# Local attention: the key and query norm roots are emitted one projection tile after their sums, the key root's broadcast another tile on

## The chip, the cores and the metric

The kernel runs on one core of a Trainium2 chip. The metric is device time in microseconds (us) from launch to end, lower is better. The inputs are float32; products run on TensorE in pieces (a rounded high part and the remainder), so each product of two matrices is three matmuls.

## What is computed

The reference is a two-layer encoder trunk over 16 meta tokens and 1024 tokens. The part that matters here is the local (windowed) attention of the first layer: 8 query heads in 2 key groups, each head of width 128, with an RMS norm of every query and key row before the attention.

```python
def swa_mixer(q_s, k_s, v_s, g_qn, g_kn, sink, cos, sin):
    ...
    q = apply_rope(rms_norm(q, g_qn), cos, sin)
    k = apply_rope(rms_norm(k, g_kn), cos, sin)
    q = q.reshape(B, SWA_KV_HEADS, SWA_REP, T, SWA_HEAD_DIM)
    o = banded_window_attention(q, k, v, sink, SWA_HEAD_DIM ** -0.5)
```

The kernel does not norm the rows before the rotation. It rotates the raw projections, sums their squares over the head's 128 features on TensorE, takes the root of the sums, and multiplies it in later: the key root as a full row over the rotated keys, the query root as a column that scales the scores.

## The kernel before

The residual stream lies transposed, features on the partitions and 1040 tokens along the free dimension. The stage of interest begins at line 524. A projection tile is `proj1(e)` (line 273): 128 output features, two halves of the weights, 36 matmuls a half, into three PSUM banks that have one buffer each in this stage. The next tile can start on a bank only when the tile before has been copied out of it. `tick()` is called inside `proj1`, behind the matmuls of the second half: it counts down the list `todo` and emits what `put_off(n, fn)` laid in it n ticks earlier. `flush()` (line 215) ticks until the list is empty.

`k_prep(g)` (line 546) projects the keys of a group: copy out of PSUM (L327, ScalarE), square (L552), scale by the norm weights on GpSimd (L553), `stat` (line 178, high and low part of the squares; its `later()` holds the sum on TensorE L197, the copies L198 and the store L199 to a row in DRAM), and `rope` (line 402: two loads of the swapped halves L405 and L406, then three full-width multiplies and adds L407 to L409). `q_prep(u)` (line 619) does the same for two heads, folds the squares of both (L439, L440, L641), and casts each rotated head to its high and low part (L633, L634).

The root of a key row is `row_rsqrt` (line 319): load the sums as 16 x 65 (L321), add the epsilon (L322), eleven small VectorE instructions of a Newton iteration (L136 to L141), store (L324). `fin2` (line 561) then loads the root broadcast to 128 partitions (`rkb`, L152) and multiplies the keys by it (L563); `put` makes the keys' high and low parts (L570 to L573). The root of a query pair is `fin` in `q_prep` (line 644): four small loads (L148, L297), L651, the same iteration on 128 x 17, and L653; the scores instruction (L694) reads the result.

Full-width rows in this stage come from one pool tag `T` with four buffers: the raw projections `kraw` and `qraw`, the swapped halves `sw`, the copied sums `sr`, the broadcast root `rkb`, and the gate rows `gt` and `gth`.

The order of emission is v, keys of group 0, query pair 0, gate tile 0, `flush()`, `put` of group 0; then 36 units of attention (four pairs of nine blocks) with the remaining projection tiles pulled in between them, 4.6 credit a unit against 5.3 a half tile (line 816: query pair 1, gate 1, query pair 2, keys of group 1, gate 2, query pair 3, gates 3 to 9). `flush()` and the `put` of group 1 stand ahead of unit 18.

The framework that builds the program chooses the order of each engine's queue at compile time. The emission order is the priority in that choice, no fixed order: the scales of the other attention (emitted behind gate tile 0) and the `put` of group 0 stand in the trace ahead of work that was emitted before them. A buffer of a tag is handed out in its own order.

Of the kernel before, what the change touches and what calls it, by code (L numbers as in the profile page):

```python
# [41 lines left out]
def trunk_kernel(ctx: ExitStack, tc: tile.TileContext, a: dict, out: bass.AP):  # L42
# [29 lines left out]
    def row(nm, tag, dt=F32, w=T):  # L72
        if tag == "X":
            return xapool.tile([P, T], dt, tag="X", name=nm)
        return sb["P"].tile([P, w], dt, tag=tag, name=nm, bufs=sb["cnt"][tag])
# [5 lines left out]
    def vcol(j):  # L81
        return vec[:, j:j + 1]
# [49 lines left out]
    def newton_rsqrt(v, shape, nm):  # L132
        y = small.tile(shape, F32, tag="nw_y" + nm, name="nw_y", bufs=1 if nm in ("72", "65", "9") else 2)
        t = small.tile(shape, F32, tag="nw_t" + nm, name="nw_t", bufs=1)
        yi = y.bitcast(I32)
        nc.vector.tensor_scalar(yi, v.bitcast(I32), 1, None, ALU.logical_shift_right)  # L136
        nc.vector.tensor_scalar(yi, yi, -1, 1597463007, ALU.mult, ALU.add)
        for _ in range(3):
            nc.vector.tensor_mul(t, y, y)
            nc.vector.scalar_tensor_tensor(t, t, -0.5, v, ALU.mult, ALU.mult)  # L140
            nc.vector.scalar_tensor_tensor(y, t, 1.5, y, ALU.add, ALU.mult)  # L141
        return y
# [4 lines left out]
    def tok_load(dst, r):  # L147
        nc.sync.dma_start(dst, r[NM:T].rearrange("(i p) -> p i", p=P))  # L148

    def bcast_row(r, nm, tag):  # L150
        t = row(nm, tag)
        nc.sync.dma_start(t, r.to_broadcast([P, T]))  # L152
        return t
# [24 lines left out]
    def stat(sq, s, m, dst, tag=None, rt="S"):  # L178

        hi = row("sqh", rt, F32R)  # L180
        lo = row("sql", rt, F32R)
        nc.gpsimd.tensor_scalar(hi, sq, 1.0, 1.0, ALU.mult, ALU.mult)
        nc.vector.tensor_sub(lo, sq, hi.bitcast(F32))

        def later():
            sr = row("sr", "T")
            if tag is None:
                ps = big("st")
                for j, x in enumerate((hi, lo)):
                    for c0, c1 in CH:  # L190
                        nc.tensor.matmul(ps[:m, OFF + c0:OFF + c1], s, x[:, c0:c1], start=j == 0, stop=j == 1)
                nc.scalar.copy(sr[:m], ps[:m, OFF:OFF + T])
            else:
                for c0, c1 in C3:
                    ps = bank("st", tag)
                    for j, x in enumerate((hi, lo)):
                        nc.tensor.matmul(ps[:m, :c1 - c0], s, x[:, c0:c1], start=j == 0, stop=j == 1)  # L197
                    nc.scalar.copy(sr[:m, c0:c1], ps[:m, :c1 - c0])  # L198
            nc.sync.dma_start(dst, sr[:m])  # L199

        return later
# [3 lines left out]
    def put_off(n, fn):  # L205
        todo.append([n, fn])
# [66 lines left out]
    def proj1(e):  # L273
        ps = parts("pj")
        for hf in range(2):
            wh, wl = split_w(a["w1"][e, hf], (4, P), "w1")
            mm3p(ps, [(wh[:, k], wl[:, k], xh[4 * hf + k], xl[4 * hf + k]) for k in range(4)], hf == 0, hf == 1)
            if hf == 1:
                tick()
            yield 5.3 if hf == 0 else ps  # L280
# [15 lines left out]
    def meta_col(dst, r):  # L296
        nc.sync.dma_start(dst, r[0:NM].unsqueeze(1))  # L297
# [21 lines left out]
    def row_rsqrt(src, n, dst):  # L319
        t16 = small.tile([16, 65], F32, tag="t16", name="t16", bufs=2)  # L320
        nc.sync.dma_start(t16, flat(src))  # L321
        nc.vector.scalar_tensor_tensor(t16, t16, 1.0 / n, e16, ALU.mult, ALU.add)  # L322
        y16 = newton_rsqrt(t16, [16, 65], "16")
        nc.sync.dma_start(flat(dst), y16)  # L324

    def take(ps, r, dve=False):
        evac(ps, lambda t, c: nc.vector.tensor_copy(r[:, c], t) if dve else nc.scalar.copy(r[:, c], t))  # L327
# [74 lines left out]
    def rope(raw, half, C, S, tag="T", eng=nc.vector):  # L402
        sw = row("sw", tag)
        for b in range(0, P, 2 * half):
            nc.sync.dma_start(sw[b:b + half], raw[b + half:b + 2 * half])  # L405
            nc.sync.dma_start(sw[b + half:b + 2 * half], raw[b:b + half])  # L406
        eng.tensor_mul(sw, sw, S)  # L407
        nc.vector.tensor_mul(raw, raw, C)
        nc.vector.tensor_add(raw, raw, sw)  # L409
# [27 lines left out]
    def fold(r, j, t0, t1):  # L437

        nc.scalar.activation(t0[64 * j:64 * j + 64], r[0:64], AF.Square)  # L439
        nc.scalar.activation(t1[64 * j:64 * j + 64], r[64:128], AF.Square)  # L440
# [97 lines left out]
    def steps(g, res):  # L538

        for v in g:  # L540
            if isinstance(v, float):
                yield v
            else:
                res.append(v)

    def k_prep(g):
        o = []
        yield from steps(proj1(6 + g), o)
        raw = row("kraw", "T")
        take(o[0], raw)  # L550
        sq = row("ksq", "S")
        nc.scalar.activation(sq, raw, AF.Square)  # L552
        nc.gpsimd.tensor_scalar(raw, raw, vcol(V_SK), 1.0, ALU.mult, ALU.mult)  # L553
        sk = stat(sq, one, 1, d_sk[g], "s")
        rope(raw, 64, sC, sS, eng=nc.gpsimd)

        def fin():
            sk()
            row_rsqrt(d_sk[g], 128, d_rks[g])

        def fin2():
            rkb = bcast_row(d_rks[g], "rkb", "T")
            nc.vector.tensor_mul(raw, raw, rkb)  # L563

        def put():
            kh = swa.tile([P, NB, 144], F32R, tag="kh", name="kh")
            kl = swa.tile([P, NB, 144], F32R, tag="kl", name="kl")
            real = raw[:, NM:T].rearrange("p (b c) -> p b c", b=NB)
            meta = raw[:, 0:NM].unsqueeze(1).to_broadcast([P, NB, NM])
            nc.scalar.copy(kh[:, :, NM:144], real)  # L570
            nc.scalar.copy(kh[:, :, 0:NM], meta)
            nc.vector.tensor_sub(kl[:, :, NM:144], real, kh[:, :, NM:144].bitcast(F32))
            nc.vector.tensor_sub(kl[:, :, 0:NM], meta, kh[:, :, 0:NM].bitcast(F32))  # L573
            KV[g, "k"] = (kh.rearrange("p b c -> p (b c)"), kl.rearrange("p b c -> p (b c)"))

        put_off(1, fin)
        put_off(2, fin2)
        KV[g, "put"] = put
        yield 5.3

# [38 lines left out]
    def q_prep(u):  # L619
        qs = []  # L620
        t0, t1 = row("qs0", "S"), row("qs1", "S")
        meta = swa.tile([P, 2, 32], F32R, tag="qm", name="qm", bufs=2)
        for r in range(2):
            o = []
            yield from steps(proj1(8 + 2 * u + r), o)
            raw = row("qraw", "T")
            take(o[0], raw)
            fold(raw, r, t0, t1)
            nc.gpsimd.tensor_scalar(raw, raw, vcol(V_SQ), 1.0, ALU.mult, ALU.mult)
            rope(raw, 64, sC, sS, eng=nc.gpsimd if u else nc.vector)  # L630
            h = row("sqh_", "q", F32R)
            lo = row("sql_", "q", F32R)
            nc.scalar.copy(h, raw)  # L633
            nc.vector.tensor_sub(lo, raw, h.bitcast(F32))  # L634
            nc.scalar.copy(meta[:, 0, NM * r:NM * r + NM], raw[:, 0:NM])
            nc.vector.tensor_sub(meta[:, 1, NM * r:NM * r + NM], raw[:, 0:NM],
                                 meta[:, 0, NM * r:NM * r + NM].bitcast(F32))
            qs.append((h, lo))
            if r == 0:
                yield 5.3  # L640
        nc.gpsimd.tensor_add(t0, t0, t1)  # L641
        sq2 = stat(t0, sel, 2, d_sq[u], "s")

        def fin():
            sq2()
            sc = small.tile([P, 17], F32, tag="ssc", name="ssc", bufs=2)
            nc.vector.memset(sc[:, 16:17], 1.0)
            for r in range(2):
                tok_load(sc[:, 8 * r:8 * r + 8], d_sq[u][r])
                meta_col(sc[NM * r:NM * r + NM, 16:17], d_sq[u][r])  # L650
            nc.vector.scalar_tensor_tensor(sc, sc, 1.0 / 128, evx_s, ALU.mult, ALU.add)  # L651
            y = newton_rsqrt(sc, [P, 17], "17")
            nc.vector.tensor_scalar(sc, y, 128.0 ** -0.5, None, ALU.mult)  # L653
            QQ[u] = (qs, meta, sc)

        put_off(1, fin)
        yield 5.3

    class Unit:
# [151 lines left out]
    for _ in chain(v_prep(), k_prep(0), q_prep(0), gate_tile(0)):  # L811
        pass
# [373 lines left out]
    class Lru:  # L1186
# [87 lines left out]
        def root(self):  # L1274
            tz = self.tz
            nc.scalar.activation(tz, tz, AF.Sqrt, scale=0.25)
# [358 lines left out]
```

## Time and profile before

| | us |
|---|---|
| median of three timed runs | 1867.83 (1867.34 to 1867.99) |
| the profiled execution's own time | 1866.78 |
| its span, first to last instruction | 1864.9 |
| TensorE busy in the span | 1803.3 (97%) |
| VectorE busy | 1229.8 (66%) |
| ScalarE busy | 877.3 (47%) |
| GpSimd busy | 802.1 (43%) |

A row of a timeline reads: start, duration, engine and line, operation, output and input names, shapes, and in brackets the idle time of that engine just before with what ended it. In a table by stretches each engine has its busy time and its instruction count, PEclk is the granted TensorE clock as a share of full speed. PEld is the weight load of TensorE, SPq the queue that issues DMAs.

### The profile page before, as it was taken

The page shows a single profiled execution, that of the slowest core. Times are in us where ns is not written, and L with a number is a line of the kernel's source. Part 1 is how long each engine was busy: PE and PEld are TensorE (multiplying, and loading weights), DVE is VectorE, ACT ScalarE, POOL GpSimd, SP SyncE. Part 2 cuts the span into 40 slices and gives each one's busy share as a digit, 9 for nine tenths or more (in the row PEclk, how much of TensorE's full clock was granted, in tenths as well). Part 3 has the DMA queues.
Part 4 walks back from the last instruction along what each step waited for, and adds up shares of the span by engine and source line. Part 5 has one row for each costly group of instructions (what it writes and reads, how often), then busy time and mean ns, then how long its engine had stood idle before and what let it go on. Part 6 is the DMA issues. An engine that isn't in the chain of part 4 may idle for free.

```text
span 1864.9 us, 28561 instructions
## 1 busy us (share of the span) xinstructions
PE 1803.3 (97%) x10822; PEld 1641.8 (88%) x10822; DVE 1229.8 (66%) x1956; ACT 877.3 (47%) x1490; POOL 802.1 (43%) x713
## 2 busy tenths in 40 slices
PE   8999989989999999999999999999999999999999
PEld 7997888889999999888888889998888889988887
DVE  8687357787764641678777774348988989989000
ACT  5455224445443210466667652127776676674000
POOL 5446365354322463357555433332433433326331
PEclk9999999999999999999999999999999999999999
DMA  5355532223222363323222103422222222136421
GB/s 181 81 191 185 164 92 69 62 60 103 61 84 93 137 184 115 117 69 93 70 75 75 41 24 117 145 70 60 76 80 74 95 72 77 60 131 254 143 77 41
DMA packets 109333, 186.47 MB, mean 100 GB/s; under 512 B 31951, under 2 KB 51535, under 8 KB 109198
## 3 DMA queue, kind: packets, MB, share of 16 engines
q1 hardware_dynamic: 109198, 184.67, 31.2%
q8 instruction: 85, 1.39, 0.3%
q14 instruction: 50, 0.41, 0.1%
HBM read 126.72 MB, written 49.92 MB: 95 GB/s over the span
## 4 chain that ended last, share of the span: by engine, by line
PE 69%; DVE 16%; ACT 7%; POOL 5%; issue 2%; DMA 1%; SPq 0%; DVEq 0%; POOLq 0%; ACTq 0%
PE pj L168 12%; PE oo L168 10%; PE pxop L168 6%; PE pg L1183 5%; PE px L935 5%; PE pu L1183 5%; PE av L1026 4%; PE tp L998 3%; PE op L168 3%; PE up L168 3%; PE pz L128 2%; PE vps L435 2%; PE py L935 2%; DVE oxl L769 1%; DVE oz L1287 1%
## 5 line engine op out<-in xcount | busy, mean ns | idle before, releaser
L116 POOL TENSOR_TENSOR wl<-wr,wh 128x512 fp32r<-128x512 f32 (+2 forms) x218 | 320.8, 1475 | 301.9 <-ACT wh L113 269.8
L115 POOL TENSOR_SCALAR wh<-wr 128x512 fp32r<-128x512 f32 (+2 forms) x157 | 121.6, 775 | 376.0 <-PE pj L168 124.4
L168 PE MATMUL pj<-xh,wl 128*128 128x346 f32 (+1 forms) x768 | 251.3, 328 | 14.3 <-DVE wl L116 7.8
L168 PE MATMUL pj<-xl,wh 128*128 128x346 f32 (+1 forms) x768 | 249.1, 324 | 0.9 <-DVE xl L269 0.8
L168 PE MATMUL pj<-xh,wh 128*128 128x346 f32 (+1 forms) x768 | 248.9, 324 | 0.0
L168 PEld LDWEIGHTS pj<-xh,wl 128*128 128x128 f32 x768 | 146.5, 191 | 16.1 <-ACT xh L268 7.7
L168 PEld LDWEIGHTS pj<-xl,wh 128*128 128x128 f32 x768 | 146.6, 191 | 2.0 <-DVE xl L269 1.9
L168 PEld LDWEIGHTS pj<-xh,wh 128*128 128x128 f32 x768 | 146.6, 191 | 0.1
L1183 PE MATMUL pu<-h1h,wl 128*128 128x346 f32 (+1 forms) x384 | 125.2, 326 | 6.3 <-DVE ou L1201 3.3
L1183 PE MATMUL pu<-h1l,wh 128*128 128x346 f32 (+1 forms) x384 | 123.5, 322 | 0.0
L1183 PE MATMUL pu<-h1h,wh 128*128 128x346 f32 (+1 forms) x384 | 123.4, 321 | 0.0
L1013 ACT CAST pth<-tp 128x512 fp32r<-128x512 f32 (+1 forms) x160 | 77.9, 507 | 66.2 <-PE tp L998 52.3
L1014 DVE TENSOR_TENSOR ptl<-tp,pth 128x512 fp32r<-128x512 f32 (+1 forms) x160 | 90.2, 585 | 19.9 <-ACT pth L1013 16.4
L1183 PE MATMUL pg<-h1h,wl 128*128 128x512 f32 x256 | 101.4, 396 | 0.0
L168 PE MATMUL oo<-oyh,wh 128*128 128x512 f32 x256 | 101.1, 395 | 0.0
L1183 PE MATMUL pg<-h1h,wh 128*128 128x512 f32 x256 | 101.1, 395 | 0.0
L1183 PE MATMUL pg<-h1l,wh 128*128 128x512 f32 x256 | 100.8, 394 | 0.0
L168 PE MATMUL oo<-oyh,wl 128*128 128x512 f32 x256 | 100.6, 393 | 0.0
L168 PE MATMUL oo<-oyl,wh 128*128 128x512 f32 x256 | 100.4, 392 | 0.0
L944 ACT ACTIVATE p<-py,mmx,msc 128x256 f32<-128x256 f32 (+1 forms) x72 | 40.8, 567 | 119.0 <-DVE mmx L942 102.3
L1351 DVE TENSOR_TENSOR hres<-oo,hres 128x512 f32<-128x512 f32 x16 | 10.6, 688 | 129.0 <-PE oo L168 129.0
L998 PE MATMUL tp<-ident,p 128*128 128x128 f32 (+1 forms) x576 | 90.5, 275 | 2.7 <-POOL p L955 1.9
(446 smaller groups left out, 5471.2 us busy)
## 6 DMA issues: line engine op xcount, KB each, us to landing
wr<-in_w SPq DMA_DIRECT2D x128, 256.0 KB
wr<-in_wo SPq DMA_DIRECT2D x64, 256.0 KB
s_g<-gth SPq DMA_DIRECT2D x10, 520.0 KB
xr<-in_x SPq DMA_DIRECT2D x8, 520.0 KB
s_qn<-qr SPq DMA_DIRECT2D x8, 520.0 KB
s_kn<-kr SPq DMA_DIRECT2D x8, 520.0 KB
sw<-qraw SPq DMA_DIRECT2D x16, 260.0 KB
yb<-s_yb SPq DMA_DIRECT2D x8, 520.0 KB
```

The source lines that it names most:

```text
L115: eng.tensor_scalar(hi[:, :n], raw[:, :n], 1.0, 1.0, ALU.mult, ALU.mult)
L116: eng.tensor_sub(lo[:, :n], raw[:, :n], hi[:, :n].bitcast(F32))
L128: nc.tensor.matmul(ps[:m, off + c0:off + c1], w, x[:, c0:c1], start=first and j == 0 and pi == 0, stop=last and j == nt - 1 and pi == 2)
L168: nc.tensor.matmul(t[:, :c1 - c0], w, x[:, c0:c1], start=first and j == 0 and pi == 0, stop=last and j == nt - 1 and pi == 2)
L435: nc.tensor.matmul(ps[:m, :n], s, w, start=j == 0 and pi == 0, stop=j == nt - 1 and pi == 2)
L935: nc.tensor.matmul(dst[:m, d0:d0 + a1 - a0], l[:, s], r[:, a0:a1], start=pi == 0, stop=pi == 4)
L944: nc.scalar.activation(p_[:m, b0:b1], ps, AF.Exp, bias=mx[:m, 2:3], scale=sc, accum_out=mx[:m, 3 + z:4 + z])
L998: nc.tensor.transpose(tp[:, o:o + m], p_[:m, NM + P * (kt + j):NM + P * (kt + j) + P], ident[:m, :m])
L1013: nc.scalar.copy(hi[:, :w], tp[:, :w])
L1014: nc.vector.tensor_sub(lo[:, :w], tp[:, :w], hi[:, :w].bitcast(F32))
L1026: nc.tensor.matmul(av[:, :n], l[:, vs], pts[kt][o][:, j * n:j * n + n], start=kt == 0 and j == 0 and pi == 0, stop=False)
L1183: nc.tensor.matmul(t[:, :c1 - c0], l, r[:, c0:c1], start=hf == 0 and k == 0 and pi == 0, stop=hf == 1 and k == 3 and pi == 2)
```

## The change

For the keys, `fin` (sums and root together, one tick later) is split: the sums stay one tick later, the root comes two ticks later, and the broadcast with its product moves from two ticks to three. For the queries, the sums stay one tick later and the loads, the root and its scaling move to two ticks. No instruction is added or removed.

```diff
-        def fin():
-            sk()
+        def root():
             row_rsqrt(d_sk[g], 128, d_rks[g])
...
-        put_off(1, fin)
-        put_off(2, fin2)
+        put_off(1, sk)
+        put_off(2, root)
+        put_off(3, fin2)
...
         def fin():
-            sq2()
             sc = small.tile([P, 17], F32, tag="ssc", name="ssc", bufs=2)
...
-        put_off(1, fin)
+        put_off(1, sq2)
+        put_off(2, fin)
         yield 5.3
```

## Rows read from the trace of the kernel before

**Rows 1.** Table by stretches of the stage and of what follows it: stretch, its length, busy time and instruction count of each engine, granted clock, DMA share, GB/s.
```profile
250.00:300.00 50.00, 42.70 (x257) 40.54 (x257) 32.67 (x67) 17.28 (x38) 24.04 (x20) 0.97 0.30 81
...
400.00:450.00 50.00, 46.17 (x314) 44.38 (x313) 40.50 (x108) 24.61 (x69) 19.23 (x24) 1.00 0.36 95
...
500.00:550.00 50.00, 49.70 (x340) 48.91 (x339) 31.54 (x89) 21.12 (x62) 15.16 (x23) 1.00 0.26 80
```

**Rows 2.** TensorE's timeline where query pair 0 is projected: the last matmul into the first PSUM bank of its second head, the last of that head, and the two tile starts behind it that waited.
```profile
255.56 0.32 PE L168 MATMUL pj<-xh,wh 128*128 128x348 f32 x1
...
259.38 0.32 PE L168 MATMUL pj<-xh,wh 128*128 128x346 f32 x1
264.03 0.43 PE L168 MATMUL pj<-xh,wl 128*128 128x348 f32 x1 [4.33 <-ACT qraw L327]
...
279.76 0.43 PE L168 MATMUL pj<-xh,wl 128*128 128x348 f32 x1 [1.26 <-DVE gt L783]
```

**Rows 3.** ScalarE's timeline over the same stretch: the cast of the first head and the copies of the second out of PSUM.
```profile
262.47 1.06 ACT L633 CAST sqh__2734<-qraw 128x1040 fp32r<-128x1040 f32 x1 [11.35 <-DVE qraw L409]
...
263.54 1.14 ACT L327 COPY qraw<-pj 128x348 f32<-128x348 f32 x3
```

**Rows 4.** VectorE's timeline over the same stretch: the first instruction of group 0's key root, the rotation and low part of the first head, the product with the broadcast root.
```profile
254.39 0.34 DVE L322 SCALAR_TENSOR_TENSOR t<-t,e 16x65 f32<-16x65 f32 x1 [6.80 <-DMA t<-d_sk]
...
258.49 1.22 DVE L407 TENSOR_TENSOR sw<-sw,sS 128x1040 f32<-128x1040 f32 x1
...
260.90 1.53 DVE L409 TENSOR_TENSOR qraw<-qraw,sw 128x1040 f32<-128x1040 f32 x1
263.56 1.24 DVE L634 TENSOR_TENSOR sql__2735<-qraw,sqh__2734 128x1040 fp32r<-128x1040 f32 x1 [1.13 <-ACT sqh__2734 L633]
...
264.80 1.24 DVE L563 TENSOR_TENSOR kraw<-kraw,rkb 128x1040 f32<-128x1040 f32 x1
```

**Rows 5.** SP's DMA issues over the same stretch: the load of the key sums and the broadcast of the root.
```profile
252.18 0.33 SPq L321 DMA_DIRECT2D t<-d_sk  x1
...
259.96 0.34 SPq L152 DMA_DIRECT2D rkb<-d_rks  x1
```

**Rows 6.** Table by stretches behind the wait of 4.33 us; columns as in Rows 1.
```profile
264.00:268.00 4.00, 3.97 (x16) 3.97 (x17) 2.07 (x4) 3.93 (x6) 1.04 (x1) 0.59 0.27 66
268.00:277.00 9.00, 9.00 (x58) 8.96 (x58) 7.97 (x5) 0.13 (x1) 7.29 (x5) 0.99 0.29 65
```

**Rows 7.** VectorE's timeline behind it: the keys' low part, the low part of the query squares, the rotation of the second head, the copies of gate tile 0 out of PSUM (L783).
```profile
267.97 1.23 DVE L572 TENSOR_TENSOR kl<-kraw,kh 128x1024 fp32r<-128x1024 f32 x1 [1.93 <-ACT kh L570]
...
272.68 1.64 DVE L183 TENSOR_TENSOR sql<-qs,sqh 128x1040 fp32r<-128x1040 f32 x1 [1.03 <-POOL sqh L182]
274.24 2.32 DVE L407 TENSOR_TENSOR sw<-sw,sS 128x1040 f32<-128x1040 f32 x1
...
279.20 1.35 DVE L783 SCALAR_TENSOR_TENSOR gt<-pj,rstd 128x348 f32<-128x348 f32 x3
```

**Rows 8.** Query pair 1: the first instruction of its root and the scores behind it on VectorE, and the TensorE start that waited for those scores.
```profile
344.76 1.25 DVE L651 SCALAR_TENSOR_TENSOR ssc<-ssc,evx_s 128x17 f32<-128x17 f32 x1
...
347.96 0.72 DVE L694 CUSTOM_DVE_ANT_0 sp<-sps,masks,vec 128x432 f32<-128x432 f32 x1
...
348.74 0.40 PE L693 MATMUL sps<-kh,sql__2735 128*128 128x288 f32 x1 [1.05 <-DVE smx L694]
```

**Rows 9.** Query pair 2: its root on VectorE (two instructions of one shape, 2.34 and 0.18 us) with the scores behind it, the GpSimd instruction that ran beside it, and the TensorE start that waited at the end of that chain.
```profile
404.82 0.37 DVE L651 SCALAR_TENSOR_TENSOR ssc<-ssc,evx_s 128x17 f32<-128x17 f32 x1
...
406.62 2.34 DVE L139 TENSOR_TENSOR nw_t<-nw_y 128x17 f32<-128x17 f32 x1
...
409.42 0.18 DVE L139 TENSOR_TENSOR nw_t<-nw_y 128x17 f32<-128x17 f32 x1
...
409.85 0.73 DVE L694 CUSTOM_DVE_ANT_0 sp<-sps,masks,vec 128x432 f32<-128x432 f32 x1
...
406.51 2.42 POOL L407 TENSOR_TENSOR sw<-sw,sS 128x1040 f32<-128x1040 f32 x1
...
416.40 0.32 PE L197 MATMUL st<-sqh,ones 128*1 128x346 f32 x1 [2.12 <-ACT sr L198]
```

**Rows 10.** The key chain of group 1: the first and the last instruction of its root, the low part of pair 2's second head, the product with the broadcast, the last score work of group 0 and the keys' low part on VectorE; the issue of the broadcast; two TensorE starts that waited.
```profile
424.40 0.21 DVE L322 SCALAR_TENSOR_TENSOR t<-t,e 16x65 f32<-16x65 f32 x1
...
428.73 0.22 DVE L141 SCALAR_TENSOR_TENSOR nw_y<-nw_t,nw_y 16x65 f32<-16x65 f32 x1
...
432.81 1.23 DVE L634 TENSOR_TENSOR sql__4183<-qraw,sqh__4182 128x1040 fp32r<-128x1040 f32 x1
...
435.33 1.23 DVE L563 TENSOR_TENSOR kraw<-kraw,rkb 128x1040 f32<-128x1040 f32 x1
...
438.50 0.42 DVE L742 TENSOR_TENSOR spmr<-tB,spmr 32x256 fp32r<-32x256 f32 x1
...
440.07 0.70 DVE L573 TENSOR_TENSOR kl<-kraw,kh 128x128 fp32r<-128x128 f32 x1
...
430.31 0.32 SPq L152 DMA_DIRECT2D rkb<-d_rks  x1
...
426.97 0.30 PE L728 MATMUL tA<-ident,sp 128*128 128x128 f32 x1 [1.10 <-DVE nw_t L140]
...
440.82 0.25 PE L693 MATMUL sps<-kl,qm 128*32 128x144 f32 x1 [0.61 <-DVE kl L573]
```

## The prediction

> **What bounds the kernel now.** The page's first part has TensorE busy for 1803.3 of 1864.9 us, so the time can fall only where TensorE stands idle or runs below its full clock. The table by stretches says where that is: TensorE is idle for 7.3 of 50 us in 250 to 300 and 3.8 in 400 to 450, but for 0.3 in 500 to 550 [rows 1]. All the moved instructions run between 245 and 495 us. So I read TensorE's timeline there for starts that waited, and from each followed the releaser back over ScalarE, VectorE and SP.
>
> The first wait is the largest. After query pair 0 the next tile starts 4.33 us late, because ScalarE copied the second head out of PSUM late [rows 2]. The first bank of that head was full at 255.9 [rows 2], but its copy came at 263.54, behind a cast that had waited 11.35 us for the end of the first head's rotation [rows 3]. I take the reason to be the buffers, not the cast: of the four rows of tag T one holds the keys, one the first head, one its swapped halves, and the fourth goes by emission order to the broadcast root, whose `fin2` is emitted ahead of the second head's copy though its load is issued only at 259.96 [rows 5]. The second head therefore gets the swapped halves' buffer, free at 262.43 when L409 ends [rows 4]. An idle ScalarE with a full bank in front of it is what speaks for this.
>
> The late start costs more than 4.33 us: in the 4 us behind it the granted clock is 0.59 and 16 matmuls run, where 58 in 9 us run at 0.99 [rows 6]. At that rate 26 would have run, so 10 matmuls of 0.155 us, 1.6 us, are lost to a clock that stood partly at its lower level (1.2 GHz) after the idle time. Another 1.26 us is waited for gate tile 0's copies by VectorE [rows 2].
>
> Three smaller waits stand behind a root. The root of pair 1 holds VectorE from 344.76 to 347.9 ahead of the scores, and TensorE waits 1.05 us for them [rows 8]. That of pair 2 holds it from 404.82 to 409.85, scores behind it, and 2.12 us follow at the end of that chain [rows 9]. That of group 1's keys lies between score work, with a wait of 1.10 us [rows 10]. Sum 4.3 us.
>
> **The change, part by part.** No instruction comes or goes, so the sum holds only waits.
>
> *Group 0, the buffer.* With `fin2` a tile later, the second head's copy takes the buffer of the copied sums, free when their store has landed, which the load at 252.18 had waited for [rows 5]. The copies then follow TensorE bank by bank and end some 0.45 us behind the tile's end at 259.70, at about 260.1, where they ended at 264.68 before [rows 3]. TensorE loses its 4.33 us wait and runs gate tile 0 to about 271 (72 matmuls of 0.155 us). But its copies (L783) then decide. VectorE had them at 279.20 behind the keys' low part, the query squares and the second head's rotation [rows 7]. The rotation follows the copy's chain: 4.6 us earlier, less the cast of 1.06 us [rows 3] that now falls between the copies and the squares and an estimated 0.4 us of ScalarE waiting for it: 3.1 us. Against it, the broadcast load now waits for the first head's buffer (L634's end, 264.80 [rows 4]), so the product L563 moves from 264.80 to about 267, 2.2 us later, and the keys' low part with it. If VectorE's list from L563 to L783, 14.4 us with 2.96 us of waits in it [rows 4, 7], closes those waits, L783 comes at 267 + 11.4 = 278.4 at the worst and 276.1 by the rotation at the best. Between them the rotation is nearer, because L783 stands right behind it in the list; I take 3.1 us. TensorE now idles from 271 to 276 in place of 260 to 264, so I leave the 1.6 us of slow clock where it is. Bounds: 0 (the list keeps its waits and the key product's delay eats the gain) and 7.2 (4.33 + 1.6 + 1.26).
>
> *Group 0, the order.* The root itself probably runs where it ran: VectorE had been idle for 6.80 us before it [rows 4], so lower priority has nothing to yield to. SP's load of the sums took 0.33 us to issue [rows 5], ahead of the swapped halves; for those, no longer standing behind it is worth about that, which is inside the bound.
>
> *Query pairs 1 to 3.* Their four loads and root become less urgent than one more projection tile and the units beside it, so scores go first. I count half of the 4.3 us of the three small waits, 2.1 us, keys of group 1 included, as VectorE is busy for 40.5 of 50 us there [rows 1] and its displaced 3 to 5 us fall before something else. Bounds: 4.3 gained, and 4.3 lost if the roots fall in front of work as urgent. Pair 3 has no waiting TensorE beside it (500 to 550 [rows 1]): nothing. All have a spare projection tile before their first scores.
>
> One instruction of pair 2's root took 2.34 us, its twin 0.18; it began 0.11 us behind a GpSimd multiply of 2.42 us and ended with it [rows 9]. The Trainium skill, SBUF — State Buffer, section Who interferes with whom, says that a VectorE instruction with two SBUF inputs and a GpSimd instruction that reads SBUF shut each other out for a whole instruction; this row agrees. By it a later root is no cheaper, as the other heads' swaps on GpSimd (2.4 us each by this row) stand there too: the term would be 2.1 less one such 2.2 us, near nothing.
>
> *Group 1's keys.* Here the delay has a deadline: the low part of the keys ends at 440.77 and TensorE waits 0.61 us for it [rows 10]. The broadcast is now emitted behind the raw row and the swapped halves of pair 3's first head, so those take the two rows of T that fall free first, and it gets the next, that of pair 2's second head, free when L634 ends at 434.04; its load was issued at 430.31 before [rows 10]. A load landed about 2.2 us after its issue in group 0 (L321 to L322 [rows 4, 5]), and the broadcast moves more, so I put L563 at about 436.8 and not 435.33, 1.5 us later, more if the root is pushed. TensorE has half a projection tile (36 matmuls, 5.6 us) to run meanwhile, so I count +0.7. Bounds 0 and 6.0 (worked out with the second rival).
>
> Sum: -3.1 - 2.1 + 0.7 = -4.5 us. The profiled execution took 1866.78 (span 1864.9 and 1.88 around it) and would take 1862.3; the median of the runs is 1.05 above it, so I forecast 1863.3.
>
> **The rivals.**
> *The order stays.* The compiler places an instruction when its data are there, and the emission order only breaks ties; the idle 6.80 us before L322 [rows 4] speak for it. Then the roots stay put, and of the group 0 wait only its place moves, from 260 to 271, since VectorE's list up to L783 is the limit. Time 1867.8, within 1.5. The Trainium skill, Perfetto Trace Analysis, section Identifying the Most-Contended Engine, says to work on the engine with the highest occupancy, here TensorE, and not on one at 66%; by it too the time would stay, but the 7.3 idle us in 250 to 300 [rows 1] show VectorE setting TensorE's time there.
>
> *The key root of group 1 comes too late: slower.* If the root yields to all score work of group 0, its end moves from 428.95 to the end of that work near 438.9 (L742 [rows 10]), some 10 us, and the keys with it. It decides as soon as the delay passes the 5.6 us of projection that TensorE has: 4.4 us idle, and 1.6 us of slow clock as behind the first wait [rows 6], +6.0. With nothing gained at group 0: 1873.8. For it: the 0.61 us wait shows no slack. Against it: the root takes 4.5 us for instructions of 0.2 us there (424.40 to 428.95 [rows 10]), so it already shares VectorE with score work and is not starved.
>
> *All the waits go.* If L783 goes ahead of the rotation, the bounds are reached: 7.2 + 4.3 = 11.5 less, 1856.3.
>
> **How the numbers follow.** Forecast (1860.5 to 1866) 0.45; order stays 0.24; late key root 0.21; all gone 0.10. The bound of 0.2%, about what a measurement here can tell from no change, is 3.7 us. Faster: all of the last and 0.32 of the forecast, 0.42. Same: the rest of the forecast and the order rival, 0.37. Slower: 0.21. The range is 1858.5 to 1871.5: it leaves out the far ends of the two outer rivals.
>
> **What would show it.** Right: the copies of the second head of pair 0 (L327) start near 256 to 260 without the cast ahead of them, no wait of 4.33 us, gate tile 0 copied near 276; L694 ahead of L651 near 347 and 405. Wrong: the copy still behind the cast; the next wait behind gate tile 0 longer than 5 us; the scores of unit 18 later than 446 with TensorE idle before them.

## The result and the profile after

The changed kernel takes 1872.94 us (median of 8 runs, 1871.35 to 1874.48); the kernel before took 1867.54 beside it (8 runs, 1866.74 to 1867.99). The ratio is 1.003 with a 95% interval of 1.0019 to 1.004: slower by 5.4 us (3.5 to 7.5), where 4.5 us less were forecast, and above the range of 1858.5 to 1871.5. The profiled execution took 1872.67 us with a span of 1870.9, against 1866.78 and 1864.9.

The first view to read is a table by stretches, cut at points of the program and not at equal times: from the start of the stage to the first scores of unit 0, to those of units 9, 18 and 27 (the lines L694 with 32x144), and from there to the first matmul of the stage's output product. The stretch from unit 9 to unit 27 is also shown in two parts, cut at unit 18. The first stretch stands last; it begins at the same time, 244.00, in both. Before (stretch, length, busy time and count of TensorE's matmuls, of its weight loads PEld, of VectorE, ScalarE and GpSimd, granted clock, DMA share, GB/s):

```profile
290.83:360.14 69.31, 61.70 (x397) 58.68 (x397) 54.18 (x136) 35.93 (x99) 32.22 (x37) 0.98 0.22 57
360.14:441.18 81.04, 74.09 (x493) 70.77 (x492) 65.12 (x155) 41.18 (x113) 40.32 (x43) 1.00 0.28 73
441.18:520.85 79.67, 76.11 (x499) 73.53 (x498) 56.63 (x146) 37.77 (x104) 34.55 (x40) 0.98 0.28 75
360.14:520.85 160.71, 150.20 (x990) 144.29 (x989) 121.76 (x301) 78.96 (x216) 74.87 (x82) 0.99 0.28 74
520.85:663.69 142.84, 140.44 (x920) 138.55 (x918) 81.47 (x168) 43.32 (x104) 49.02 (x56) 1.00 0.33 107
244.00:290.83 46.83, 40.60 (x244) 38.27 (x242) 27.73 (x46) 14.04 (x25) 25.20 (x17) 0.96 0.32 85
```

The same points after:

```profile
290.47:359.40 68.93, 61.81 (x397) 58.60 (x397) 53.98 (x136) 36.11 (x99) 31.69 (x37) 0.98 0.21 57
359.40:458.44 99.04, 89.06 (x583) 85.35 (x582) 70.54 (x162) 45.62 (x123) 48.13 (x48) 0.99 0.30 79
458.44:525.62 67.18, 62.72 (x408) 60.30 (x408) 53.04 (x139) 33.20 (x94) 25.74 (x35) 0.97 0.23 61
359.40:525.62 166.22, 151.78 (x990) 145.65 (x989) 123.58 (x300) 78.83 (x216) 73.87 (x82) 0.98 0.27 72
525.62:669.64 144.02, 141.36 (x919) 139.47 (x918) 81.61 (x168) 43.30 (x104) 48.83 (x56) 1.00 0.32 107
244.00:290.47 46.47, 40.17 (x239) 37.87 (x238) 30.14 (x45) 14.24 (x25) 24.75 (x17) 0.93 0.30 82
```

The two stretches up to unit 9 gain 0.36 and 0.38 us. Between units 9 and 27, where both run the same 990 matmuls, the kernel loses 166.22 - 160.71 = 5.51 us: 3.93 of it is idle time of TensorE (166.22 - 151.78 against 160.71 - 150.20) and 1.58 is longer busy time at a lower clock. Of the idle time, 3.03 us lie ahead of unit 18's first scores (9.98 against 6.95) and 0.90 behind them. The stretch from unit 27 on adds 1.18, which was not followed further.

**Group 0.** The forecast chain is there, and so is a new wait behind it (timelines of ScalarE, SP, VectorE and TensorE, in order of time):

```profile
255.04 0.45 ACT L327 COPY qraw<-pj 128x348 f32<-128x348 f32 x1 [4.80 <-PE pj L168]
...
266.94 0.34 SPq L152 DMA_DIRECT2D rkb<-d_rks  x1
...
273.44 2.30 DVE L562 TENSOR_TENSOR kraw<-kraw,rkb 128x1040 f32<-128x1040 f32 x1
...
275.88 0.78 ACT L198 COPY sr<-st 2x348 f32<-2x348 f32 x2 [13.19 <-DVE kraw L562]
276.38 0.45 PE L197 MATMUL st<-sqh,sel 128*2 128x346 f32 x1 [5.43 <-ACT sr L198]
...
276.99 1.37 DVE L783 SCALAR_TENSOR_TENSOR gt<-pj,rstd 128x348 f32<-128x348 f32 x3
```

The stretches of 3.6 and 4 us behind that wait, columns as in the first table:

```profile
276.40:280.00 3.60, 3.15 (x10) 2.50 (x11) 3.50 (x6) 2.81 (x6) 0.00 (x0) 0.50 0.11 42
280.00:284.00 4.00, 4.00 (x23) 3.95 (x23) 2.17 (x4) 1.07 (x1) 0.00 (x0) 0.80 0.18 12
```

The second head's copy comes at 255.04 behind TensorE alone, not behind the cast [rows 3], and the wait of 4.33 us [rows 2] is gone. But TensorE then waits 5.43 us for the copy of the query sums, which ScalarE could make only once the key product L562 had read its row (a row of T that the copied sums take next), and the clock behind it is 0.50, all of the time at the lower level (1.2 GHz), where it was 0.59 [rows 6]. Gate tile 0 is copied at 276.99 and not at 279.20 [rows 7]; the first scores come 0.36 us earlier. TensorE's two waits here, 4.33 and 1.26 us [rows 2], have become one of 5.43.

**Group 1.** Here the time is lost. The chain in order of time: the last instruction of the root on VectorE, the store and the loads on SP, the rotation of pair 3's first head on GpSimd and VectorE, the product, the low part, TensorE:

```profile
431.25 0.98 DVE L141 SCALAR_TENSOR_TENSOR nw_y<-nw_t,nw_y 16x65 f32<-16x65 f32 x1
433.57 0.44 SPq L324 DMA_DIRECT2D d_rks<-nw_y  x1
441.24 0.33 SPq L96 DMA_DIRECT2D wr<-in_w  x1
441.90 1.14 POOL L629 TENSOR_SCALAR qraw<-qraw,vec 128x1040 f32<-128x1040 f32 x1 [0.69 <-ACT qs L440]
443.07 0.47 SPq L405 DMA_DIRECT2D sw<-qraw  x1
443.59 0.59 SPq L406 DMA_DIRECT2D sw<-qraw  x1
444.29 0.62 SPq L152 DMA_DIRECT2D rkb<-d_rks  x1
447.56 2.29 DVE L408 TENSOR_TENSOR qraw<-qraw,sC 128x1040 f32<-128x1040 f32 x1 [3.85 <-DMA sw<-qraw]
448.71 3.44 POOL L407 TENSOR_TENSOR sw<-sw,sS 128x1040 f32<-128x1040 f32 x1
452.19 1.24 DVE L409 TENSOR_TENSOR qraw<-qraw,sw 128x1040 f32<-128x1040 f32 x1 [2.34 <-POOL sw L407]
453.35 1.23 DVE L562 TENSOR_TENSOR kraw<-kraw,rkb 128x1040 f32<-128x1040 f32 x1
455.80 1.22 DVE L571 TENSOR_TENSOR kl<-kraw,kh 128x1024 fp32r<-128x1024 f32 x1
455.91 0.33 PE L693 MATMUL sps<-kh,qm 128*32 128x144 f32 x1 [3.00 <-ACT kh L570]
458.44 0.42 DVE L694 CUSTOM_DVE_ANT_0 sp<-sps,masks,vec 32x144 f32<-32x144 f32 x1 [1.22 <-PE sps L693]
```

The waits of SP's queue between 430 and 446 (line that waited, what ended it, us in total, times, longest), and the clock behind TensorE's wait:

```profile
SPq L96 <- POOL wl L116: 13.6, 2, 7.1
```

```profile
456.00:460.00 4.00, 4.00 (x21) 3.96 (x22) 2.40 (x8) 2.59 (x5) 1.91 (x2) 0.61 0.09 35
```

The root ends 3.3 us later than in [rows 10], but the load of the broadcast is issued 14 us later (444.29 for 430.31) and the product 18 us later (453.35 for 435.33). Behind the store, SP stood at a weight load (L96) until 441.24 (the longest wait, 7.1 us, for GpSimd's weight split L116; in the kernel before, that load waits behind the broadcast's and not ahead of it), and then at the swapped halves of pair 3's first head, which wait for GpSimd's scale of that head (L629, end 443.04). The product stands on VectorE behind the rotation of the same head, and that waits for GpSimd again. TensorE has 3.0 us of idle time in place of 0.61 [rows 10], and the clock is at 0.61 behind it.

### The profile page after: what moved, and what is told of

Same layout as the page of the kernel before. It is cut to its first block, busy times and chain, and to the rows that moved or that the text cites. A ratio compares the mean times of both kernels' runs of the same rounds, so it can differ in the third digit from the quotient of the medians.

```text
span 1870.9 us, 28566 instructions
## 1 busy us (share of the span) xinstructions
PE 1806.4 (97%) x10822; PEld 1644.7 (88%) x10822; DVE 1230.5 (66%) x1956; ACT 877.4 (47%) x1490; POOL 800.8 (43%) x713
## 4 chain that ended last, share of the span: by engine, by line
PE 71%; DVE 15%; ACT 7%; POOL 5%; issue 2%; DMA 1%; SPq 0%; DVEq 0%; POOLq 0%; ACTq 0%
PE pj L168 14%; PE oo L168 9%; PE pxop L168 6%; PE pg L1183 6%; PE px L935 5%; PE pu L1183 5%; PE av L1026 4%; PE tp L998 3%; PE op L168 3%; PE up L168 3%; PE pz L128 3%; PE vps L435 2%; PE py L935 2%; DVE oxl L769 1%; DVE oz L1287 1%
## 5 line engine op out<-in xcount | busy, mean ns | idle before, releaser
L116 POOL TENSOR_TENSOR wl<-wr,wh 128x512 fp32r<-128x512 f32 (+2 forms) x218 | 323.1, 1486 | 301.8 <-ACT wh L113 265.7
```

The lines of the kernel that those rows point to most:

```text
L116: eng.tensor_sub(lo[:, :n], raw[:, :n], hi[:, :n].bitcast(F32))
```

## The experiments

Each ran in 5 rounds (5 to 11 runs) beside the kernel before; a difference in us is one of medians, and the ratio with its 95% interval stands behind it.

**Which part of the change.** Four kernels change one part alone, written as the ticks of the sums, the root and the broadcast (before 1, 1, 2; after 1, 2, 3).

*keys_only*: both key groups as after, queries as before.
```diff
-        put_off(1, fin)
-        put_off(2, fin2)
+        put_off(1, sk)
+        put_off(2, root)
+        put_off(3, fin2)
```


> The keys of both groups are changed, the query pairs are as in the kernel before. Theory (the loss is made at the keys of group 1, whose broadcast load is emitted behind the next head and so stands behind that head's swapped halves on SP): 5 us slower than the kernel before (4 to 6.5), first scores of unit 18 near 458. Rival (the loss comes from the query roots, or from group 0's new wait of 5.44 us together with them): within 1.5 us of the kernel before.

Measured: 1872.66, +4.9 us, ratio 1.0025 (1.0015 to 1.0034); unit 18's scores at 457.30.

*queries_only*: queries as after, keys as before.
```diff
-            sq2()
...
-        put_off(1, fin)
+        put_off(1, sq2)
+        put_off(2, fin)
```


> Only the query pairs' roots are moved, the keys are as in the kernel before. Theory: within 1.2 us of the kernel before, since the waits at pairs 1 to 3 changed place and not their sum (1.04, 1.15 and 0.82, 1.56 us after; 1.05, 2.12, 1.10 before). Forecast of the prediction: 2 us faster. Rival that the queries make the loss: 3 us slower or more.

Measured: 1867.44, -0.4 us, ratio 0.9997 (0.9988 to 1.0006). A gain or a loss of the queries is not shown.

*group0_keys*: keys of group 0 alone.
```diff
+        put_off(1, sk)
+        put_off(1 if g else 2, root)
+        put_off(2 if g else 3, fin2)
```


> Only the keys of group 0 are changed; the keys of group 1 and all query pairs are as before. Theory: the wait of 4.33 us goes and one of about 5.4 us comes in front of gate tile 0's sum of squares, with the clock half of full behind it: 0.4 to 1.0 us faster than the kernel before. Forecast of the prediction: 3.1 us faster. Rival that the new wait makes the loss: 2 us slower or more.

Measured: 1867.22, -0.6 us, ratio 0.9995 (0.9986 to 1.0003), with a wait of 5.85 us in front of the sums. So, by difference, the loss is all of group 1's: 4.9 + 0.6 = 5.5 us, with an interval of some 1.7 us either way on each of the two; no run has group 1's change alone.

*g1_bcast_only*: the kernel before with group 1's broadcast alone a tile later.
```diff
+        put_off(1, sk)
+        put_off(1, root)
+        put_off(3 if g else 2, fin2)
```


> The kernel before with only group 1's broadcast and product one tile later; the root is where it was. Theory (the load stands on SP behind the swapped halves that wait for GpSimd, whenever the root ends): load issued near 443, first scores of unit 18 near 457, 4.5 to 6 us slower than the kernel before, as with both moved. Rival (the late root is what costs, the broadcast only adds to it): 0 to 2.5 us slower.

Measured: 1871.50, +4.0 us, ratio 1.0025 (1.0016 to 1.0034). The root's store is as early as before and the chain ends as late as after:

```profile
428.27 0.32 SPq L324 DMA_DIRECT2D d_rks<-nw_y  x1
...
443.37 0.56 SPq L152 DMA_DIRECT2D rkb<-d_rks  x1
...
452.42 1.23 DVE L562 TENSOR_TENSOR kraw<-kraw,rkb 128x1040 f32<-128x1040 f32 x1
...
454.99 0.26 PE L693 MATMUL sps<-kh,qm 128*32 128x144 f32 x1 [2.99 <-ACT kh L570]
```

The load is issued 15 us after the store. The place of the broadcast is enough for most of the loss, 4.0 of 5.5 us (4.7 by the ratio), where 4.5 to 6 were expected; the late root isn't needed for this part.

**What the late root does alone.** *g1_bcast_with_root* is the changed kernel with `put_off(2 if g else 3, fin2)`; *g1_root_only* is the kernel before with `put_off(1, sk)` and `put_off(2 if g else 1, root)`; its broadcasts stay at two ticks.

> The changed kernel, but the broadcast of group 1 is emitted in the root's tick and not one tile on. Theory (it is the broadcast's place behind the swapped halves): its load is issued at about 435 in place of 444, the product ends near 439, unit 18's first scores come near 445, and the time is 0 to 1.5 us below the kernel before. Rival (the root, 3.3 us later by its lower place, is late enough by itself): unit 18 later than 450, and 3 us or more slower than the kernel before.

> The kernel before with only group 1's key root one tile later; its broadcast stays in the tick that it had, which is now the root's own. Theory after the run with the broadcast in the root's tick (2.7 us slower): a root 3 to 5 us later by itself moves unit 18's first scores from 441 to about 446 and costs 2.5 to 4 us. Rival (that run lost its time by where group 0 and the query roots put the rest): within 1 us of the kernel before.

Measured: 1870.52, +2.7 us, ratio 1.0013 (1.0004 to 1.0022); and 1869.79, +2.3 us, ratio 1.0008 (0.9999 to 1.0017). By its ratio the second is 1.5 us slower, and its interval takes in no change; three of its eleven runs took 1866.25 to 1867.19, the other eight 1869.52 to 1872.08. The load is issued at 436.75 and 435.08, unit 18 comes at 446.81 and 444.45, with its keys in time. So the first theory, that the broadcast's place is all, missed: it had 0 to 1.5 us below the kernel before. Its rival had unit 18 later than 450 and missed too, and the second kernel lost a little less than the 2.5 to 4 us of its theory. What TensorE waits for here is one product of 32x128 on VectorE (g1_root_only; GpSimd, VectorE, TensorE):

```profile
446.67 0.61 POOL L115 TENSOR_SCALAR wh<-wr 128x512 fp32r<-128x512 f32 x1
447.26 2.38 POOL L407 TENSOR_TENSOR sw<-sw,sS 128x1040 f32<-128x1040 f32 x1
449.61 1.25 POOL L116 TENSOR_TENSOR wl<-wr,wh 128x512 fp32r<-128x512 f32 x1
...
446.73 4.21 DVE L713 TENSOR_SCALAR sp<-sp,ssm 32x128 f32<-32x128 f32 x1 [0.54 <-POOL spm L710]
...
451.08 0.22 PE L728 MATMUL tA<-ident,sp 32*128 32x32 f32 x1 [2.91 <-DVE sp L713]
```

L713 begins 0.06 us behind the first of three GpSimd instructions in a row and ends 0.08 us behind the last of them: 4.21 us. In the kernel before it runs at 443.71, ahead of that rotation (448.15), in 0.27 us. The traced execution is one of the three short ones (1866.53, where the trace of the kernel before has 1866.78), so it shows the wait and not what the eight longer runs lost. The trace of g1_bcast_with_root (1870.76) has the same wait, 2.92 us at 453.46.

**The load's queue and the buffer.** *bcast_act_queue* is the changed kernel with ScalarE issuing the load; *bcast_S_row* takes the broadcast's row from another tag.
```diff
-            rkb = bcast_row(d_rks[g], "rkb", "T")
+            rkb = row("rkb", "T")
+            nc.scalar.dma_start(rkb, d_rks[g].to_broadcast([P, T]))
```
```diff
-            rkb = bcast_row(d_rks[g], "rkb", "T")
+            rkb = bcast_row(d_rks[g], "rkb", "S")
```


> The changed kernel with the load of the broadcast issued by ScalarE and not by SP, in the same place of the emission. Theory (SP's order holds the load): it is issued behind the copies and squares of pair 3's first head, near 442 in place of 444.3, and unit 18 comes 2 us earlier or more; 2 to 4 us slower than the kernel before. Rival (the product stands behind the rotation on VectorE whatever the load does): unit 18 near 458, 5 us slower or more.

> The changed kernel with the broadcast row taken from the pool of the squares (tag S) and not from the four rows of T. Theory: the wait in front of gate tile 0's sum of squares (5.44 us after) goes, because the copied sums no longer wait for the product's row; group 1's load is issued near 437 and no longer behind the swapped halves, so unit 18 comes near 447 as with the broadcast in the root's tick. Time 0 to 3 us above the kernel before. Rival (the loss is the order on VectorE alone, not the load): unit 18 still near 458, 4 us slower or more.

Measured: 1874.06, +6.5 us, ratio 1.0035 (1.0022 to 1.0047); and 1873.96, +6.4 us, ratio 1.0032 (1.002 to 1.0045). Both theories missed. The times are those of the rivals, but unit 18 comes at 455.22 and 455.82, not near 458. Both edits move group 0's load as well (the first scores of all come at 287.67 and 291.39, for 290.47 after), so these times are not group 1's alone. With ScalarE's queue the load is 3 us earlier and the product 8 us, but the low part then falls beside GpSimd's rotation product:

```profile
441.21 0.33 ACTq L562 DMA_DIRECT2D rkb<-d_rks  x1
445.47 1.24 DVE L563 TENSOR_TENSOR kraw<-kraw,rkb 128x1040 f32<-128x1040 f32 x1 [1.62 <-DMA rkb<-d_rks]
...
448.88 3.49 POOL L407 TENSOR_TENSOR sw<-sw,sS 128x1040 f32<-128x1040 f32 x1
450.00 3.44 DVE L572 TENSOR_TENSOR kl<-kraw,kh 128x1024 fp32r<-128x1024 f32 x1
...
454.86 0.25 PE L694 MATMUL sps<-kl,qm 128*32 128x144 f32 x1 [3.13 <-DVE kl L573]
```

Unit 18 comes 3.2 us earlier than in the changed kernel and unit 27 1.8 us later (527.43 for 525.62); the waits between them were not followed.

With the row from another tag, SP still takes the load only behind the weight load:

```profile
441.76 0.33 SPq L96 DMA_DIRECT2D wr<-in_w  x1
442.20 0.37 SPq L152 DMA_DIRECT2D rkb<-d_rks  x1
```

Group 1 ends much the same way (product at 446.92, a VectorE product of 3.44 us beside GpSimd's 3.39, two waits of 2.04 and 2.00 us), and at group 0 the wait moves once more:

```profile
278.52 0.66 PE L168 MATMUL pj<-xh,wl 128*128 128x348 f32 x1 [6.09 <-DVE gt L783]
```

So at group 0 the broadcast's row of T is not the only bound: with it out of the way TensorE waits for VectorE's list up to L783, and the first scores come at 291.39.

**GpSimd's product beside the keys.** These kernels do the sine product (L407) of pair 3's first head on VectorE. *before_rot_vec*, *after_rot_vec*, *g1_root_rot_vec* and *act_queue_rot_vec* apply it to the kernel before, the changed one, g1_root_only and bcast_act_queue.
```diff
-            rope(raw, 64, sC, sS, eng=nc.gpsimd if u else nc.vector)
+            rope(raw, 64, sC, sS, eng=nc.vector if u == 0 or (u, r) == (3, 0) else nc.gpsimd)
```


> The control: the kernel before with the same rotation product on VectorE. There GpSimd's product takes 3.44 us beside a VectorE product of 2.32 us and nothing waits for it on TensorE, so the time stays within 1.2 us of the kernel before.

> The changed kernel with the sine product of the rotation of pair 3's first head done by VectorE (about 1.2 us) and not by GpSimd (3.44 us after). Theory (a good part of the delay of the keys is that rotation, for which VectorE waited 2.34 us and beside which its products took 2.3 us for 1.2): the product begins 2 to 3 us earlier, near 450.5, unit 18 near 455, and the time is 2 to 3 us less than that of the changed kernel, 2 to 3.5 us above the kernel before. Rival (only the queue order counts): no gain over the changed kernel, 5 us above the kernel before.

> The changed kernel with the broadcast's load issued by ScalarE (ahead of the swapped halves) and the sine product of pair 3's first head on VectorE: both the order on SP and the GpSimd instruction beside the keys' low part are gone. Theory (what is left of the loss with the early load is the low part, 3.44 us for 1.23, shut out by GpSimd's product): the low part takes about 1.2 us, unit 18 comes near 452 and the time is 0 to 2 us above the kernel before. Rival (the load on ScalarE costs by itself): 4 us slower or more, as with the load on ScalarE alone.

> Only group 1's key root one tile later (broadcast in the same tick), with that sine product on VectorE. Theory (the run with the late root alone lost its 1.5 us to one small product, L713, of 4.21 us beside three GpSimd instructions in a row, one of them this sine product): L713 takes under 2 us, TensorE's wait of 2.9 us behind it is under 1.5, and the time is within 1 us of the control with the sine product on VectorE (1866.06). Rival (the root's 3 us by themselves): 1.5 us or more above that control.

Measured: before_rot_vec 1866.06, -1.7 us, ratio 0.9992 (0.9983 to 1.0001); after_rot_vec 1870.17, +2.4 us, 1.0014 (1.0005 to 1.0022); act_queue_rot_vec 1869.06, +1.1 us, 1.0004 (0.9995 to 1.0013); g1_root_rot_vec 1866.86, -1.1 us, 0.9994 (0.9985 to 1.0003). The control itself was forecast within 1.2 us of the kernel before and came 1.7 below it. After_rot_vec took the time that was forecast, but with the product at 452.31 and unit 18 at 457.77, not near 450.5 and 455 (its root starts 1.4 us later than the changed kernel's). Against the control, before_rot_vec, the full change costs 4.1 us, with the early load 2.8, the late root alone 0.6. Each of these is the difference of two differences that have intervals of some 1.7 us either way, so the last is not told from nothing. In g1_root_rot_vec, L713 is back to 0.63 us and the wait of 2.91 us is gone; in act_queue_rot_vec the low part takes 1.22:

```profile
448.34 0.63 DVE L713 TENSOR_SCALAR sp<-sp,ssm 32x128 f32<-32x128 f32 x1 [0.54 <-POOL spm L710]
```

```profile
445.87 1.24 DVE L563 TENSOR_TENSOR kraw<-kraw,rkb 128x1040 f32<-128x1040 f32 x1 [1.57 <-DMA rkb<-d_rks]
...
451.59 1.22 DVE L572 TENSOR_TENSOR kl<-kraw,kh 128x1024 fp32r<-128x1024 f32 x1
...
454.22 0.25 PE L694 MATMUL sps<-kl,qm 128*32 128x144 f32 x1 [0.91 <-DVE kl L573]
```

With the early load, taking the product off GpSimd is worth 5.4 us (6.5 to 1.1), clear of the noise and of the 1.7 us that it is worth in the kernel before. The early load alone gained nothing (6.5 for 5.4), and with the product off GpSimd it may gain 1.3 us (4.1 to 2.8), which is inside the noise. That the order of the queues and the stretched instructions are in series, so that either holds the chain when the other is taken away, fits the rows but is argued and not shown by the times. The 2.8 us that are left were not taken apart further; unit 18 comes at 454.58 and not at the 452 that I expected, because two products of that head's rotation (L407 at 449.28, L408 at 450.44) stand on VectorE between the keys' product and their low part.

**With slack.** *keys1_earlier* and its control *before_keys1_earlier* project the keys of group 1 ahead of query pair 2, in the changed kernel and in the one before.
```diff
-    jobs = chain(q_prep(1), gate_tile(1), q_prep(2), k_prep(1), gate_tile(2), q_prep(3),
+    jobs = chain(q_prep(1), gate_tile(1), k_prep(1), q_prep(2), gate_tile(2), q_prep(3),
```


> The changed kernel with the keys of group 1 projected one place earlier (ahead of query pair 2), so that the moved broadcast has two projection tiles more before unit 18. Theory (the broadcast came behind the next head with no slack left): its load is issued ahead of 425, unit 18's first scores are back near 441, and the time is 1 us below to 1 us above the kernel before. Rival (the late root and broadcast disturb the scores wherever they fall): 3 us slower or more.

> The control: the kernel before with the same projection order (keys of group 1 ahead of query pair 2). The order by itself: within 1.5 us of the kernel before. If the changed kernel in this order is within 1 us of this control, the change costs nothing where there is slack.

Measured: 1870.46 and 1869.73, both with a ratio of 1.0013 (1.0004 to 1.0022); against the kernel before both are above what was forecast. The order of projection costs 2 us by itself (a wait of 3.15 us at 373.69 in the control is new); the change on top costs 0.7 us, inside the 1 us that was forecast and less than the runs can tell from nothing. The load is issued at 380.08 and the product begins at 384.96, 59 us before unit 18's scores. Where there is slack, a cost of the same edit is not shown.

**A version to keep.** *g0_rot_vec* is group0_keys with the one sine product on VectorE; *g0_rot_vec23* has those of all heads of pairs 2 and 3 there (`eng=nc.gpsimd if u == 1 else nc.vector`).

> A version to keep: only group 0's keys are changed (broadcast and root a tile later, 0.6 us gained alone), and that sine product is on VectorE (1.7 us gained alone). If the two add up: 1.5 to 2.5 us below the kernel before. Rival (both gain by the same drop of the clock near 470): 1 to 1.7 us below.

> As the version to keep, but the sine products of all heads of pairs 2 and 3 on VectorE. If GpSimd's long products are what stretches VectorE's small ones: a further 0.5 to 1.5 us less. Rival (VectorE, busy for 40.5 of 50 us in 250 to 300 and nearly so beside the units, is the fuller engine): 0.5 us or more slower than with the one product moved.

Measured: 1865.84, -2.1 us, ratio 0.9991 (0.9982 to 1.0); and 1865.99, -1.9 us, ratio 0.9990 (0.9981 to 0.9999). Both lie below both kernels, at the edge of what the runs can tell from the kernel before; more heads on VectorE bring nothing more, against both forecasts. The first lies in its forecast of 1.5 to 2.5, but before_rot_vec has 1.7 of it alone, so a gain from group 0's keys is not shown.

## Why the prediction was wrong

*The term that failed: group 1's keys.* It forecast +0.7 us, with 6.0 as its upper bound; it measured 5.5 (keys_only less group0_keys). The step put the product L563 at 436.8, from the row of T and the root, and it came at 453.35. What the step left out is the load's own queue. It names the swapped halves as emitted ahead of the load, but draws from that only which row the load gets; it did not ask what stands on SP between the store and the moved load: a weight load and those swapped halves, each waiting for GpSimd. The row did not decide: the read that it named, L634, ends at 434.96 after the change, and SP took the load only at 444.29; without a row of T (bcast_S_row) it came at 442.20, behind the same weight load. The 2.2 us from issue to landing, read from a smaller load, were too short as well: in the runs where VectorE waits for the broadcast, the product begins 3.7 to 4.7 us behind the issue. The step also left out that the product's turn on VectorE moves behind the rotation, and that the later the chain, the nearer it falls to GpSimd's product of 3.44 us. g1_bcast_only shows that the broadcast's place alone makes most of the loss. How much of that is SP's queue and how much VectorE's order is not shown: with the load on ScalarE's queue unit 18 came 3.2 us earlier and no time was gained.

*The slower rival.* It gave 1873.8, 0.9 us from the measured time, and that is in part luck. Its price was of the right kind: TensorE waits for the keys of unit 18, 3.00 us for 0.61, and the slow clock behind that costs 4.00 x 0.39 = 1.6 us in 456 to 460. Its reason is refuted: the root is 3.3 us later, not 10, and the late root alone costs 0.6 us, not told from nothing, once GpSimd's product is away. That it decides at TensorE's 5.6 us of projection was too early as well: unit 18 came 17.3 us later and TensorE idled 3.0 us before it, since the projection tiles of later heads filled in: of the 990 matmuls, 583 now run before unit 18's scores and 408 after them, where it was 493 and 499 (matmuls at the cut count on both sides). Of the 0.90 us of idle time behind unit 18, waits of 0.66 us at 474.83 and 1.42 at 491.89 are new, and one of 0.56 at 458.15 is gone; that of 1.90 at 468.14 is not, it was 1.79 at 468.60. That the missing projection makes them is argued, not shown.

*Group 0, the buffer.* The mechanism was right: the copy comes at 255.04, and the wait of 4.33 us is gone in group0_keys too (which moves root and broadcast; they were not tried apart). The load did get the first head's row: SP waits 2.2 us for VectorE's last read of it (L636, end 266.91). The gain was mis-sized: 3.1 forecast, 0.6 us measured by group0_keys (interval -2.6 to +0.6). The step put the key product near 267 and it came at 273.44, behind the query squares and two products of the second head's rotation; and it did not see that the copy of the query sums would wait for that product's row, with TensorE behind it. L783 came at 276.99, 2.2 us earlier, so the list of VectorE did shrink by most of what I took; but leaving the slow clock at 1.6 us was wrong: it grew with the wait (5.43 for 4.33) to some 3.15 x 0.50 + 4.00 x 0.20 = 2.4 us. That the wait only changes its place, as the rival of the unmoved order had it, is nearer to what happened, and bcast_S_row shows the list of VectorE behind it.

*Query pairs.* Forecast -2.1, measured -0.4 (interval -2.2 to +1.1). At pair 1 the root, but for its last instructions, stayed in front of the scores and the wait is 1.05 us as before [rows 8]; at pair 2 the root went behind, the wait of 2.12 us [rows 9] became 1.15, and 0.82 came at 420.23. The lower value named there, near nothing, fits better; whether for the reason given there was not tried. The interval just takes in the forecast.

*The signs.* Of those named for right, the early copy and the gate tile near 276 came, and scores ahead of the root near 405 but not near 347. Of those named for wrong, two came: a wait of more than 5 us behind gate tile 0, and unit 18 later than 446 with TensorE idle before it.

## What to carry to other kernels

A load that is emitted later can be later by the waits of whatever is emitted ahead of it on its queue, not by the delay of its data: here by 14 us, with data that were 3.3 us late. Before such a move, list the queue between the old and the new place, and what each entry waits for. Where two engines slow each other's instructions, look for the long instruction that a delayed chain will run into. The change as a whole costs 5.4 us where the moved chain has no slack, and 0.7 us, not told from nothing, where it has (keys1_earlier): look for the slack of each group before moving both.

## What the runs showed of the hardware

A VectorE product of 32x128 took 4.21 us, held through three GpSimd instructions in a row, and 0.63 in g1_root_rot_vec, where only the first of the three stood beside it:

```profile
448.28 0.61 POOL L115 TENSOR_SCALAR wh<-wr 128x512 fp32r<-128x512 f32 x1
```

In both it ends 0.08 us behind the last GpSimd instruction beside it. The Trainium skill, SBUF — State Buffer, section Who interferes with whom, says that of two instructions that contend for the shared ports the one that issues first keeps them for its whole length and the other is blocked; the rows of g1_root_only agree, and show the VectorE instruction blocked for three in a row, without a turn between them.

A wait of one length can have either clock behind it. g1_root_rot_vec waits 1.46 us up to 467.89 and runs the first of these stretches at 0.59, most of the time at the lower level (1.2 GHz); before_rot_vec waits 1.50 us up to 467.18 and runs the second at full clock:

```profile
467.89:471.89 4.00, 3.60 (x15) 3.42 (x16) 3.39 (x6) 0.96 (x2) 3.92 (x3) 0.59 0.21 70
```

```profile
467.18:471.18 4.00, 3.60 (x24) 3.44 (x25) 3.40 (x6) 0.86 (x2) 3.92 (x3) 1.00 0.20 63
```

In the 6 us ahead of these stretches TensorE was busy for 4.54 and 4.50 us, with 30 matmuls in each, at full clock. So the length of this wait doesn't set the clock here, and what does is open. The kernel before (a wait of 1.79 us up to 468.60) has 0.61 in the 4 us behind it, which before_rot_vec has not; but g0_rot_vec has 0.65 there (a wait of 1.50 us) and is no slower than before_rot_vec. The drop is therefore not shown to make the 1.7 us that before_rot_vec gains, and the cause of these stays open.
